# First layer's modulation vectors summed on VectorE, 512-column attention splits, new durations in the schedule

## The chip, the cores and the metric

The kernel runs on one core of a Trainium2 chip. The metric is the device time of one execution in microseconds (us). The kernel before took 1266.96 us, the median of three runs (1266.91 to 1268.06). The profiled execution, from which all rows below come, took 1268.53 us, of which the trace spans 1266.7 us. The names of the engines are those of the profile: PE is TensorE's matmul (PEld its weight load), DVE is VectorE, ACT is ScalarE, POOL is GpSimd, SP issues the DMAs.

## The reference

Two layers of a diffusion backbone over 256 latent tokens and 256 context tokens, 1024 wide. Each layer has a mixing half (three branches: windowed attention with 8 query and 2 key heads, a multi-scale pooling, a gated linear recurrence in two directions; merged by sigmoid gates) and a SwiGLU half. In the second layer only the latent tokens are carried to the end. What matters for the change:

```
mod_x = silu(c)     @ w_ada[l] + b_ada[l]     # 6 vectors of 1024, for the latent stream
mod_c = silu(c_ctx) @ w_ada[l] + b_ada[l]     # the same 6, for the context stream
h  = rms_norm(x, g_pre) * (1 + mod[1]) + mod[0]         # mixing half; vectors 4 and 3 in the SwiGLU half
x  = x + mod[2] * rms_norm(mix, g_post_mix)             # vector 5 in the SwiGLU half
p  = softmax(q k^T + mask, sink)                        # per head; 256 or 512 keys
o  = p v
h_t = a_t * h_(t-1) + b_t                               # the recurrence, forward and backward
```

All inputs and the output are float32.

## The kernel before

**Matmuls.** A float32 product is made of three reduced-precision products: each operand is split into a high part (`whi`, `h`, `b`, rounded to fp32r) and the rest (`wlo` for weights), and PE multiplies high by high, high by rest and rest by high. For weights ACT makes `whi` from the loaded tile `raw` and DVE makes `wlo = raw - whi` (`split_w`); one such pair of 128x1024 feeds 24 matmuls of 512 columns in the first layer. Activations are split in the same way by `hilo` (ACT the high part, DVE the rest). PSUM has two tags of four banks: `pm` for the large products, `pa` for everything else.

**The modulation vectors.** For one half (512 wide) of one vector, eight tiles of `w_ada` (`ra`, 128x512, eight buffers) are loaded. There are two ways to sum them. `ada_acc` does it on DVE: for each tile and each stream one SCALAR_TENSOR_TENSOR, `acc = ra * csilu + acc`; the 128 partial sums of a column, one in each partition, are then added either by four PE transposes and a DVE TENSOR_REDUCE (`ada_columns`, for vectors that are needed as columns) or by two fp32r matmuls with a matrix of ones (`ada_gate`, for the gates, after a `hilo`). `ada_rows` does it on PE: eight float32 matmuls with 32 columns of weights (`ra` with `cT`), four of them side by side in the array by `tile_position`; a DVE addition of the bias gives `ar`, and small float32 matmuls bring it into columns (`row_columns`) or spread it over the partitions (`row_gate`, with the constant `spread`). The kernel before uses `ada_rows` for six half-vectors of the first layer (vectors 3, 4 and 2), for both streams at once, and `ada_acc` for the fourteen half-vectors that are worked on in the first layer's SwiGLU half (vector 5 of the first layer, all of the second). A half-vector is one job; `tick` starts its next load between products.

**Attention.** A unit is one block of 128 queries, one pair of heads `jp` and one key head `g`: `attn_scores` (products, row maximum, exponential), `attn_trans` (scaling by the reciprocal of the sum, transposes into PSUM, `hilo` of the result), `attn_pv`. Units follow each other as a side stream beside the merge of a branch. `attn_trans` takes one `pa` bank for each of the two heads `jj` and splits it in pieces of 256 columns. The queries are split in pieces of 64 partitions by 128 columns.

**The order of the work.** No engine's order is written by hand. Every call is recorded with an estimated duration (`price`); `schedule` then plays all engines in time and fixes the order in each queue: whichever recorded operation is ready and has the lowest number comes first. Side work (recurrence, pooling, attention) is recorded with its number raised by `SIDE[l]`. On the chip each engine then works through its fixed queue in order, waiting by semaphores. The durations of `price` are thus nothing but a rule for the order. The call that issues everything stands in one line (L420), so all rows of the profile have that line.

Of the kernel before, what the change touches and what calls it, by code (L numbers as in the profile page):

```python
# [15 lines left out]
ALU = mybir.AluOpType  # L16
# [86 lines left out]
class Program:  # L103
# [114 lines left out]
    def price(self, op, method, args, kw, writes, reads):  # L218
# [10 lines left out]
        elif op.eng == "tensor":  # L229
            dt = kw["lhsT"].dtype if method == "matmul" else F32  # L230
            if method == "transpose":
                op.cost = max(n, 32) * 0.83e-3
            elif dt == F32R:
                op.cost = 0.1077 if n == 256 else 0.2145
            elif dt == BF16:
                op.cost = n * 0.4167e-3
            else:
                op.cost = max(n * 1.667e-3 / (4 if "tile_position" in kw else 1), 0.106)
# [195 lines left out]
class Builder:  # L434
# [14 lines left out]
    PAD = 80  # L449
# [50 lines left out]
    def load_constants(self, consts):  # L500
# [24 lines left out]
        self.spread = self.const([128, 2, 128], F32, "spread")  # L525
        nc.vector.tensor_copy(self.spread, self.c[:, C_SUM:C_SUM + 2].unsqueeze(2).to_broadcast([128, 2, 128]))
# [154 lines left out]
    def ada_rows(self, l, m, h, done):  # L681

        nc, w = self.nc, self.I["w_ada"][l]
        c0 = m * D + h * 512
        nc.sync.dma_start(out=self.brow[BIAS:BIAS + 1, :], in_=self.I["b_ada"][l:l + 1, c0:c0 + 512])
        raws, landings = [], []
        for k in range(8):
            raws.append(self.sb("ra", [128, 512], F32, "ra"))
            landings.append(nc.sync.dma_start(out=raws[k], in_=w[k * 128:(k + 1) * 128, c0:c0 + 512]))
            if k < 7:  # L690
                yield
        ps = self.ps("pa")
        for k in range(8):
            j = k % 4
            nc.after = landings
            nc.tensor.matmul(ps[32 * j:32 * j + 32, :], lhsT=self.cT[:, k, :], rhs=raws[k], start=k < 4, stop=k >= 4,
                             tile_position=(0, 32 * j))
            nc.after = []
        ar = self.sb("acc", [128, 512], F32, "acc")
        nc.vector.tensor_tensor(out=ar, in0=ps, in1=self.brow, op=ALU.add)  # L700
        done(ar)
        yield

    def row_columns(self, l, m, h, mods, g):
        def done(ar):
            nc = self.nc
            dst = mods[m % 3][:, h * 4:(h + 1) * 4, :]
            pc = self.ps("pa")
            for i in range(4):
                nc.tensor.matmul(pc[:, 2 * i:2 * i + 2], lhsT=ar[:, i * 128:(i + 1) * 128], rhs=self.c[:, C_SUM:C_SUM + 2],  # L710
                                 start=True, stop=True)
            p3 = pc[:, 0:8].rearrange("p (i s) -> p i s", s=2)
            if m % 3 == 0:
                nc.vector.tensor_copy(dst, p3)
            else:
                nc.vector.scalar_tensor_tensor(out=dst, in0=p3, scalar=1.0, in1=self.col(l, g, h * 4, 4).unsqueeze(2).to_broadcast([128, 4, 2]),
                                               op0=ALU.add, op1=ALU.mult)
        return self.ada_rows(l, m, h, done)

# [3 lines left out]

    def row_gate(self, l, m, h, g_post, streams, ggs):
        def done(ar):
            nc = self.nc
            for s in streams:
                gg, landing = self.gate_tile(l, h, g_post)
                ps = self.ps("pa")
                nc.after = [landing]  # L730
                nc.tensor.matmul(ps, lhsT=self.spread[:, s], rhs=ar, start=True, stop=True)
                nc.after = []
                nc.vector.tensor_tensor(out=gg, in0=ps, in1=gg, op=ALU.mult)
                ggs[s, h] = gg
        return self.ada_rows(l, m, h, done)
# [114 lines left out]
    SIDE = (40, 80)  # L850
# [241 lines left out]
    def q_out(self, ps, sl, full):  # L1092
        q = self.single(full, "q")
        self.nc.scalar.activation(q[:, sl], ps[:, sl], AF.Copy, scale=HD ** -0.5)
        self.rope(q)
        return q

# [31 lines left out]
    def attn_trans(self, st):  # L1129
# [4 lines left out]
        nkt = nk // 128  # L1134
        pts = [[self.T(dt=F32R).rearrange("p (k j q) -> p k j q", k=2, j=2) for _ in range(nkt // 2)] for _ in range(2)]
        for jj in range(2):
            p = st["p"][jj]
            nc.scalar.activation(p, p, AF.Copy, scale=rd[:, jj:jj + 1])
            ps = self.ps("pa")
            for kt in range(nkt):  # L1140
                nc.tensor.transpose(ps[:, kt * 128:(kt + 1) * 128], p[:, kt * 128:(kt + 1) * 128], self.ident)
            for i in range(nkt // 2):
                src = ps[:, i * 256:(i + 1) * 256].rearrange("p (k q) -> p k q", k=2)
                self.hilo(pts[0][i][:, :, jj, :], pts[1][i][:, :, jj, :], src)
# [16 lines left out]
    def attention(self, l, qtoks, q, kg, vg, outs):  # L1161
# [16 lines left out]
        for i in range(n + 2):  # L1178
            if i < n:
                qt, jp, g = units[i]  # L1180
                if (jp, g) == (0, 0):
                    sl = slice(qt * 128, (qt + 1) * 128)
                    two = (self.T(dt=F32R), self.T(dt=F32R))
                    qs = [[t[:, j * 128:(j + 1) * 128] for j in range(4)] for t in two]
                    for j in range(4):
                        for h in range(2):
                            a, b = slice(h * 64, (h + 1) * 64), slice((1 - h) * 64, (2 - h) * 64)
                            self.hilo(qs[h][j][a], qs[h][j][b], q[j][:, sl][a])
                state[i] = self.attn_scores(l, qt, jp, g, qs, kg)
# [225 lines left out]
    def layer_mix(self, l, hT, first):  # L1415
# [105 lines left out]
        for jp in range(2):  # L1521
            wq = self.q_weights(w_in, jp)
            for jj in range(2):
                ps = self.ps()
                self.gemm(ps, wq[jj], hT, sl)
                q[2 * jp + jj] = self.q_out(ps, sl, full)
# [260 lines left out]
```

## Time and profile before

| what | value |
|---|---|
| median of three runs | 1266.96 us |
| profiled execution | 1268.53 us |
| its span | 1266.7 us |
| PE busy | 1236.7 us (98%) |
| DVE busy | 866.6 us (68%) |
| ACT busy | 661.8 us (52%) |
| POOL busy | 36.4 us (3%) |
| moved by DMA | 200.45 MB, mean 158 GB/s |

How to read the rows below. A row of a group gives the engine, the operation, the tiles as out<-in, the shape and the count, then the busy time, the mean length of one, and the idle time just before with what ended it. Records of instructions that follow each other on one engine overlap a little, so a run of them is shorter than its count times the mean. In a row of the timeline, equal instructions are merged: start, length of the run, count. The first layer's mixing half lies at about 50 to 450 us, its SwiGLU half from there to about 830, the second layer after that.

### The profile page before, as it was taken

To read this page: it belongs to the slowest core of one execution; us is meant where nothing else is said; L and a number is where in the kernel's file an instruction comes from. 1 tells how busy PE (TensorE), PEld (TensorE's weight loads), DVE (VectorE), ACT (ScalarE), POOL (GpSimd) and SP (SyncE) were. 2 spreads that over 40 slices of the span, in tenths; PEclk is the share of its full clock that TensorE was granted. 3 is DMA by queue.
4 is the path that set the end of the run, shared out by engine and by line. 5 is a ranking of instruction groups with operands and counts; after the bars stand their busy time and mean duration, and the time that the engine had idled before them with its cause. 6 is when DMAs were issued, how large, how long until landed. Compare 5 with 4: busy or idle time off the path is not lost.

```text
span 1266.7 us, 17100 instructions
## 1 busy us (share of the span) xinstructions
PE 1236.7 (98%) x6175; PEld 1011.9 (80%) x6175; DVE 866.6 (68%) x1513; ACT 661.8 (52%) x1199; POOL 36.4 (3%) x95
## 2 busy tenths in 40 slices
PE   6999999999999999999999999999999999999997
PEld 3787877787778888888888888899876787888886
DVE  2587577778686389468477933478789977566743
ACT  4645668568633383222223322375789976566532
POOL 1000000000000020000000000120000000000000
PEclk9999999999999999999999999999999999999999
DMA  9744344343365446355658834325542475466662
GB/s 333 241 117 150 97 145 129 118 142 105 100 207 173 125 153 207 100 164 179 207 180 266 269 95 121 101 84 160 161 138 83 117 216 176 136 186 188 195 197 69
DMA packets 216700, 200.45 MB, mean 158 GB/s; under 512 B 12916, under 2 KB 171924, under 8 KB 216616
## 3 DMA queue, kind: packets, MB, share of 16 engines
q1 hardware_dynamic: 216616, 199.36, 50.9%
q8 instruction: 48, 0.79, 0.3%
q14 instruction: 36, 0.29, 0.1%
HBM read 196.18 MB, written 3.15 MB: 157 GB/s over the span
## 4 chain that ended last, share of the span: by engine, by line
PE 59%; DVE 3%; ACT 2%; issue 1%; POOL 0%; DVEq 0%; POOLq 0%; ACTq 0%
PE pm L420 47%; PE pa L420 11%; DVE t L420 1%; ACT t L420 1%; DVE wlo L420 1%; ACT junk_a L420 0%; DVE b L420 0%; POOL s L420 0%; DVE junk_v L420 0%; DVE h L420 0%; ACT hx L420 0%; ACT whi L420 0%; ACT b L420 0%; DVE hx L420 0%; ACT L420 0%
## 5 line engine op out<-in xcount | busy, mean ns | idle before, releaser
L420 PE MATMUL pm<-h,whi 128*128 128x512 f32 (+1 forms) x2096 | 609.2, 370 | 1.1 <-ACT whi L420 0.6
L420 DVE TENSOR_TENSOR wlo<-raw,whi 128x1024 fp32r<-128x1024 f32 (+1 forms) x263 | 311.2, 1187 | 189.8 <-ACT whi L420 180.4
L420 PEld LDWEIGHTS pm<-h,whi 128*128 128x128 f32 x2096 | 378.4, 190 | 70.7 <-issue 4.3
L420 PE MATMUL pm<-h,wlo 128*128 128x512 f32 (+1 forms) x1192 | 407.9, 343 | 1.4 <-DVE wlo L420 1.4
L420 ACT ACTIVATE whi<-raw 128x1024 fp32r<-128x1024 f32 (+1 forms) x263 | 268.9, 1029 | 265.5 <-PE pm L420 142.6
L420 PEld LDWEIGHTS pm<-h,wlo 128*128 128x128 f32 x1192 | 225.6, 189 | 29.2 <-DVE wlo L420 1.8
L420 PE MATMUL pm<-whi,b 128*128 128x512 f32 x456 | 165.3, 392 | 1.7 <-ACT b L420 1.7
L420 PE MATMUL pa<-whi,b 128*128 128x512 f32 x360 | 132.7, 390 | 0.0
L420 ACT ACTIVATE tm<-pm 128x512 f32<-128x512 f32 (+1 forms) x98 | 49.0, 503 | 123.2 <-PE pm L420 123.1
L420 DVE SCALAR_TENSOR_TENSOR acc<-ra,csilu,acc 128x512 f32<-128x512 f32 x140 | 101.6, 748 | 2.0 <-DMA ra<-in_w_ada_dram 0.3
L420 PEld LDWEIGHTS pm<-whi,b 128*128 128x128 f32 x456 | 85.4, 188 | 19.9 <-ACT b L420 2.5
L420 PE MATMUL pm<-wlo,b 128*128 128x512 f32 x228 | 89.4, 392 | 1.1 <-DVE wlo L420 1.1
L420 PEld LDWEIGHTS pa<-whi,b 128*128 128x128 f32 x360 | 67.4, 188 | 13.9
L420 PE MATMUL pm<-whi,h 128*128 128x512 f32 x224 | 77.0, 408 | 0.6 <-ACT whi L420 0.6
L420 PE MATMUL pa<-wlo,b 128*128 128x512 f32 x180 | 70.2, 390 | 0.0
L420 PE MATMUL pm<-b,whi 128*128 128x512 f32 x192 | 60.7, 394 | 0.0
L420 PE MATMUL pa<-consts,t 128*128 128x128 f32 x280 | 45.2, 284 | 8.3 <-DVE t L420 7.8
L420 PEld LDWEIGHTS pm<-wlo,b 128*128 128x128 f32 x228 | 42.9, 188 | 10.2 <-DVE wlo L420 1.6
L420 PEld LDWEIGHTS pm<-whi,h 128*128 128x128 f32 x224 | 41.9, 189 | 10.2 <-ACT whi L420 1.2
L420 PEld LDWEIGHTS pa<-consts,t 128*128 128x128 f32 x280 | 34.0, 145 | 19.6 <-DVE t L420 7.6
L420 DVE TENSOR_TENSOR t<-pa,t 128x256 fp32r<-128x256 f32 (+1 forms) x104 | 40.2, 418 | 11.8 <-ACT t L420 10.7
L420 POOL TENSOR_SCALAR s<-s 128x1 f32<-128x1 f32 x26 | 15.2, 584 | 1100.3 <-ACT junk_a L420 1094.3
(180 smaller groups left out, 1353.7 us busy)
## 6 DMA issues: line engine op xcount, KB each, us to landing
raw<-in_w_in_dram SPq DMA_DIRECT2D x84, 512.0 KB
ra<-in_w_ada_dram SPq DMA_DIRECT2D x160, 256.0 KB
raw<-in_w_gu_dram SPq DMA_DIRECT2D x80, 512.0 KB
raw<-in_w_down_dram SPq DMA_DIRECT2D x44, 512.0 KB
b<-in_w_ada_dram SPq DMA_DIRECT2D x32, 256.0 KB
raw<-in_w_out_dram SPq DMA_DIRECT2D x16, 512.0 KB
raw<-in_w_pool_o_dram SPq DMA_DIRECT2D x8, 512.0 KB
raw<-in_w_rnn_o_dram SPq DMA_DIRECT2D x8, 512.0 KB
```

The source lines that it names most:

```text
L420: op.fn(*op.args, **op.kw)
```

## The change

Six things are changed. (1) The six jobs of the first layer that used `ada_rows` now use `ada_columns` and `ada_gate`, as all others did; `ada_rows`, `row_columns`, `row_gate` and `spread` are gone. (2) `attn_trans` puts both heads of a unit into one set of banks and splits 512 columns at a time. (3) The queries are split for two blocks at once (`split_q`), and in the second layer two heads are rotated at once (`q_pair`). (4) `price` takes (n + 32) / 2400 us for an fp32r matmul of n columns (0.1200 for 256 and 0.2267 for 512, before 0.1107 and 0.2175) and twice the former time per column for a scan. (5) `SIDE` of the second layer goes from 80 to 40. (6) The pad in SBUF grows by 256 columns, which is the size of the constant that is gone.

```
-                op.cost = 0.1077 if n == 256 else 0.2145
+                op.cost = (n + 32) / 2400 - 0.003
...
+            if method == "tensor_tensor_scan":
+                per *= 2
...
-    PAD = 80
+    PAD = 336
...
-        self.spread = self.const([128, 2, 128], F32, "spread")
-        nc.vector.tensor_copy(self.spread, self.c[:, C_SUM:C_SUM + 2].unsqueeze(2).to_broadcast([128, 2, 128]))
...
-    SIDE = (40, 80)
+    SIDE = (40, 40)
...
+    def q_pair(self, pss):
+        q = self.B()
+        for jj in range(2):
+            nc.scalar.activation(q[:, jj * 256:(jj + 1) * 256], pss[jj][:, 256:TOK], AF.Copy, scale=HD ** -0.5)
...
+        nc.vector.stream_shuffle(sw, q, [(i + 16) % 32 for i in range(32)])
+        nc.vector.tensor_tensor(out=s3, in0=s3, in1=sin, op=ALU.mult)
...
+    def split_q(self, q, qt, full):
+            if full:
+                tiles = [self.T(dt=F32R) for _ in range(2)]
+                for j in range(4):
+                    dst = tiles[j // 2][:, j % 2 * 256:j % 2 * 256 + 256]
+                    self.hilo(dst[a], dst[b], q[j][:, qt * 128:qt * 128 + 256][a])
+            else:
+                tiles = [self.sb("ra", [128, 512], F32R, "qs") for _ in range(2)]
+                for jp in range(2):
+                    self.hilo(tiles[jp][a], tiles[jp][b], q[2 * jp][a])
...
+        banks = [self.ps("pa") for _ in range(n)]
         for jj in range(2):
             p = st["p"][jj]
             nc.scalar.activation(p, p, AF.Copy, scale=rd[:, jj:jj + 1])
-            ps = self.ps("pa")
...
-                self.hilo(pts[0][i][:, :, jj, :], pts[1][i][:, :, jj, :], src)
+            for kt in range(2 * n):
+                o = kt % 2 * 256 + jj * 128
+                nc.tensor.transpose(banks[kt // 2][:, o:o + 128], p[:, kt * 128:(kt + 1) * 128], self.ident)
+        for i in range(n):
+            self.hilo(*(pts[e][i].rearrange("p k j q -> p (k j q)") for e in range(2)), banks[i])
...
-                if (jp, g) == (0, 0):
+                if (jp, g) == (0, 0) and qt % 2 == 0:
+                    both = self.split_q(q, qt, len(qtoks) == 4)
...
-                    self.jobs.append(self.row_columns(0, m, h, self.mods, "g_pre_ffn"))
+                    self.jobs.append(self.ada_columns(0, m, h, streams, self.mods, "g_pre_ffn"))
...
-                self.jobs.append(self.row_gate(0, 2, h, "g_post_mix", streams, self.ggs))
+                self.jobs.append(self.ada_gate(0, 2, h, "g_post_mix", streams, self.ggs))
```

What this does to the queues is shown at three places. The first is PE in the first layer, at the end of the first job of six; `pm_316` and `pm_317` are the same large product, `acc_259` and `acc_260` the sums for the two streams. Before:

```order
L420 MATMUL pm_316<-h_224,wlo_319 128x512
L420 MATMUL pa_323<-ra_259,cT 32x512
L420 MATMUL pa_323<-ra_271,cT 32x512
L420 MATMUL pa_323<-ra_277,cT 32x512
L420 MATMUL pa_323<-ra_283,cT 32x512
L420 MATMUL pa_323<-ra_290,cT 32x512
L420 MATMUL pa_323<-ra_302,cT 32x512
L420 MATMUL pa_323<-ra_313,cT 32x512
L420 MATMUL pa_323<-ra_322,cT 32x512
L420 MATMUL pa_326<-t_314,whi_261 128x512
L420 MATMUL pa_326<-t_315,whi_261 128x512
```
After:

```order
L422 MATMUL pm_317<-h_223,whi_319 128x512 x2
L422 MATMUL pm_317<-h_223,wlo_320 128x512
L422 MATMUL pa_324<-consts,acc_260 128x128 x4
L422 MATMUL pa_325<-consts,acc_259 128x128 x4
L422 MATMUL pa_326<-t_315,whi_262 128x512
L422 MATMUL pa_326<-t_316,whi_262 128x512
L422 MATMUL pa_326<-t_315,wlo_263 128x512
```
The eight matmuls with `cT` have become eight transposes at the same place in the queue; the four matmuls of two columns that followed a few rows further on are gone.

The second place is DVE in the same stretch, before PE gets there: pooling (`t`), weight splits (`wlo`) and, after the change, the sums of the first job. Before:

```order
L420 TENSOR_TENSOR wlo_275<-raw_273,whi_274 128x1024
L420 TENSOR_TENSOR t_267<-t_258 128x2x270
L420 SCALAR_TENSOR_TENSOR t_247<-t_246,cols,t_247 128x512
L420 TENSOR_TENSOR wlo_281<-raw_279,whi_280 128x1024
L420 TENSOR_TENSOR t_268<-t_267 128x2x268
L420 TENSOR_TENSOR wlo_287<-raw_285,whi_286 128x1024
L420 TENSOR_TENSOR t_269<-t_268 128x2x264
L420 TENSOR_TENSOR t_270<-t_269 128x2x256
L420 TENSOR_TENSOR wlo_299<-raw_297,whi_298 128x1024
L420 TENSOR_TENSOR t_270<-t_270,consts 128x2x8 x2
L420 SCALAR_TENSOR_TENSOR t_247<-t_246,cols,t_247 128x512
```
After:

```order
L422 TENSOR_TENSOR wlo_282<-raw_280,whi_281 128x1024
L422 TENSOR_TENSOR t_269<-t_268 128x2x268
L422 TENSOR_TENSOR wlo_288<-raw_286,whi_287 128x1024
L422 TENSOR_TENSOR t_270<-t_269 128x2x264
L422 SCALAR_TENSOR_TENSOR acc_259<-ra_291,csilu,acc_259 128x512
L422 TENSOR_TENSOR t_271<-t_270 128x2x256
L422 SCALAR_TENSOR_TENSOR acc_260<-ra_291,csilu,acc_260 128x512
L422 TENSOR_TENSOR t_271<-t_271,consts 128x2x8 x2
L422 TENSOR_TENSOR wlo_300<-raw_298,whi_299 128x1024
L422 SCALAR_TENSOR_TENSOR t_283<-t_271,t_257 128x512
L422 SCALAR_TENSOR_TENSOR acc_259<-ra_303,csilu,acc_259 128x512
L422 SCALAR_TENSOR_TENSOR acc_260<-ra_303,csilu,acc_260 128x512
```
The sums stand between the weight splits, one or two at a time, the two streams in turn.

The third place is DVE in the second layer, at the second group of scans of the recurrence (the listing names a scan SCALAR_TENSOR_TENSOR; here it is those that read a `b` tile, such as `t_1861<-b_1868,t_1862`; `junk_v` is the row maximum of attention). Before:

```order
L420 TENSOR_TENSOR wlo_1983<-raw_1981,whi_1982 128x1024
L420 TENSOR_SCALAR junk_v,s_1916<-pa_1918,nsink 128x512
L420 SCALAR_TENSOR_TENSOR t_1896<-t_1902,t_1896 128x512
L420 TENSOR_SCALAR junk_v,s_1916<-pa_1920,nsink 128x512
L420 TENSOR_TENSOR t_1862<-t_1862,t_1861 128x512
L420 TENSOR_TENSOR t_1871<-t_1871,t_1870 128x512
L420 TENSOR_TENSOR t_1891<-t_1891,t_1890 128x512
L420 TENSOR_TENSOR t_1897<-t_1897,t_1896 128x512
L420 SCALAR_TENSOR_TENSOR t_1861<-b_1868,t_1862 128x512
L420 SCALAR_TENSOR_TENSOR t_1870<-b_1877,t_1871 128x256
L420 SCALAR_TENSOR_TENSOR t_1890<-b_1894,t_1891 128x512
```
After:

```order
L422 TENSOR_TENSOR wlo_1964<-raw_1962,whi_1963 128x1024
L422 SCALAR_TENSOR_TENSOR t_1897<-t_1903,t_1897 128x512
L422 TENSOR_TENSOR t_1863<-t_1863,t_1862 128x512
L422 TENSOR_TENSOR t_1872<-t_1872,t_1871 128x512
L422 TENSOR_TENSOR t_1892<-t_1892,t_1891 128x512
L422 TENSOR_TENSOR t_1898<-t_1898,t_1897 128x512
L422 SCALAR_TENSOR_TENSOR t_1862<-b_1869,t_1863 128x512
L422 SCALAR_TENSOR_TENSOR t_1871<-b_1878,t_1872 128x256
L422 SCALAR_TENSOR_TENSOR t_1891<-b_1895,t_1892 128x512
L422 SCALAR_TENSOR_TENSOR t_1871<-b_1878,t_1871,t_1872 128x256
L422 SCALAR_TENSOR_TENSOR t_1897<-b_1902,t_1898 128x256
```
Before, two row maxima of attention stand between the weight split and the scans; after, they stand behind them (from the fifth row below the piece on), and two weight splits that stood ahead of the scans now follow them: 173 splits of the whole queue stand ahead instead of 175. In both orders the next weight split after the one shown follows 24 or 25 rows further on.

## Rows read from the trace of the kernel before

**Rows 1.** the page: busy us, share of the span, instructions of each engine
```profile
PE 1236.7 (98%) x6175; PEld 1011.9 (80%) x6175; DVE 866.6 (68%) x1513; ACT 661.8 (52%) x1199; POOL 36.4 (3%) x95
```

**Rows 2.** stretches of the span: us, busy us (count) by engine, clock, DMA share, GB/s
```profile
50.00:450.00 400.00, 397.52 (x1919) 317.50 (x1919) 284.93 (x581) 233.58 (x459) 6.46 (x16) 1.00 0.44 135
350.00:400.00 50.00, 50.00 (x225) 39.28 (x224) 41.94 (x57) 16.78 (x22) 0.00 (x0) 1.00 0.56 175
475.00:825.00 350.00, 349.95 (x1593) 290.38 (x1592) 223.15 (x291) 98.87 (x135) 6.00 (x14) 1.00 0.55 171
900.00:1000.00 100.00, 94.84 (x427) 70.06 (x426) 87.60 (x180) 88.89 (x158) 0.00 (x0) 1.00 0.38 121
```

**Rows 3.** PE groups by form: busy us, mean ns | idle before
```profile
L420 PE MATMUL pa<-ra,cT 128*32 128x512 f32 x96 | 11.5, 598 | 0.0
L420 PE MATMUL pa<-acc,spread 128*128 128x512 f32 x8 | 3.8, 592 | 0.0
L420 PE MATMUL pa<-consts,acc 128*128 128x2 f32 x32 | 3.9, 244 | 0.7 <-DVE acc L420 0.7
L420 PE MATMUL pa<-consts,acc 128*128 128x128 f32 x48 | 6.7, 272 | 0.0
L420 PE MATMUL pa<-t,ones 128*128 128x512 f32 x16 | 4.3, 389 | 0.0
```

**Rows 4.** PE in order of time, around one removed group: start us, us
```profile
302.52 1.92 PE L420 MATMUL pa<-ra,cT 128*32 128x512 f32 x16
304.37 0.39 PE L420 MATMUL pa<-t,b 128*128 128x256 f32 x1
```

**Rows 5.** DVE groups by form, columns as in group 3
```profile
L420 DVE SCALAR_TENSOR_TENSOR acc<-ra,csilu,acc 128x512 f32<-128x512 f32 x140 | 101.6, 748 | 2.0 <-DMA ra<-in_w_ada_dram 0.3
L420 DVE TENSOR_REDUCE sc_m<-pa 128x4 f32<-128x512 f32 x4 | 2.7, 687 | 3.4 <-PE pa L420 3.4
L420 DVE TENSOR_TENSOR t<-acc,t 128x512 fp32r<-128x512 f32 x8 | 5.5, 688 | 0.7 <-ACT t L420 0.7
L420 DVE TENSOR_TENSOR acc<-pa,brow 128x512 f32<-128x512 f32 x6 | 4.1, 689 | 0.3 <-PE pa L420 0.2
L420 DVE TENSOR_TENSOR t<-pa,t 128x256 fp32r<-128x256 f32 x80 | 31.0, 418 | 6.3 <-ACT t L420 5.5
L420 DVE TENSOR_TENSOR t<-b,t 64x128 fp32r<-64x128 f32 x48 | 13.5, 286 | 1.1
L420 DVE TENSOR_TENSOR t<-pa,t 64x256 f32<-64x256 f32 x24 | 10.0, 418 | 5.5 <-ACT t L420 5.2
```

**Rows 6.** DVE in order of time, runs of weighted sums: start us, us
```profile
493.72 4.06 DVE L420 SCALAR_TENSOR_TENSOR acc<-ra,csilu,acc 128x512 f32<-128x512 f32 x6
...
685.96 3.12 DVE L420 SCALAR_TENSOR_TENSOR acc<-ra,csilu,acc 128x512 f32<-128x512 f32 x4
```

**Rows 7.** the stretch 475 to 825, instructions that touch acc alone
```profile
475.00:825.00 350.00, 6.69 (x48) 5.69 (x48) 97.11 (x135) 3.15 (x5) 1.00 0.55 171
```

**Rows 8.** the SP queue's waits, whole span: us in total, times, longest
```profile
SPq L420 <- DVE acc L420: 76.1, 96, 5.8
```

**Rows 9.** DVE in order of time, second layer's second scans: start us, us
```profile
962.34 2.49 DVE L420 TENSOR_TENSOR t<-t,t 128x512 f32<-128x512 f32 x4
964.75 2.91 DVE L420 TENSOR_TENSOR_SCAN t<-b,t 128x512 f32<-128x512 f32 x3
...
970.11 0.42 DVE L420 TENSOR_TENSOR t<-t,t 128x256 f32<-128x256 f32 x1
```

**Rows 10.** PE in order of time, same place: start us, us, idle before
```profile
968.25 0.73 PE L420 MATMUL pm<-whi,h 128*128 128x512 f32 x2 [0.58 <-ACT whi L420]
970.69 0.50 PE L420 MATMUL pm<-whi,b 128*128 128x512 f32 x1 [1.70 <-ACT b L420]
```

**Rows 11.** stretches around the end of the first mixing half, columns as in group 2
```profile
456.00:460.00 4.00, 2.87 (x14) 2.67 (x14) 3.65 (x4) 3.54 (x7) 2.66 (x2) 0.71 0.67 225
460.00:464.00 4.00, 4.00 (x32) 4.00 (x32) 2.22 (x3) 2.06 (x5) 0.46 (x1) 0.87 1.00 287
```

More of the change, by code (lines that the diff above doesn't have):

```diff
@@ L679, in ada_acc @@
         yield
[L681 to L691, printed above, removed]
-        ps = self.ps("pa")
[L693 to L718, printed above, removed]
     def gate_tile(self, l, h, g_post):
@@ L722, in gate_tile @@
         return gg, self.nc.sync.dma_start(out=gg, in_=self.I[g_post][l, h * 512:(h + 1) * 512].partition_broadcast(128))
[L724 to L735, printed above, removed]
     def tick(self, n=1):
@@ L1092, in q_out @@
     def q_out(self, ps, sl, full):
-        q = self.single(full, "q")
-        self.nc.scalar.activation(q[:, sl], ps[:, sl], AF.Copy, scale=HD ** -0.5)
+        q = self.B()
+        self.nc.scalar.activation(q, ps, AF.Copy, scale=HD ** -0.5)
         self.rope(q)
         return q
+    def q_pair(self, pss):
+        nc = self.nc
+        q = self.B()
+        for jj in range(2):
+            nc.scalar.activation(q[:, jj * 256:(jj + 1) * 256], pss[jj][:, 256:TOK], AF.Copy, scale=HD ** -0.5)
+        sw = self.T()
+        cos, sin = (self.c[:, o:o + 256].unsqueeze(1).to_broadcast([128, 2, 256]) for o in (C_COS, C_SIN))
+        q3, s3 = (t.rearrange("p (j q) -> p j q", j=2) for t in (q, sw))
+        nc.vector.stream_shuffle(sw, q, [(i + 16) % 32 for i in range(32)])
+        nc.vector.tensor_tensor(out=s3, in0=s3, in1=sin, op=ALU.mult)
+        nc.vector.tensor_tensor(out=q3, in0=q3, in1=cos, op=ALU.mult)
+        nc.vector.tensor_tensor(out=q, in0=q, in1=sw, op=ALU.add)
+        return q
+    def split_q(self, q, qt, full):
+        both = []
+        for h in range(2):
+            a, b = slice(h * 64, (h + 1) * 64), slice((1 - h) * 64, (2 - h) * 64)
+            if full:
[7 more added lines that the diff above has]
+                    self.hilo(tiles[jp][a], tiles[jp][b], q[2 * jp][a])
+            both.append(tiles)
+        return both
     def attn_scores(self, l, qt, jp, g, qs, kg):
@@ L1133, in attn_trans @@
         nc.vector.reciprocal(rd, st["den"])
-        nkt = nk // 128
-        pts = [[self.T(dt=F32R).rearrange("p (k j q) -> p k j q", k=2, j=2) for _ in range(nkt // 2)] for _ in range(2)]
+        n = nk // 256
+        pts = [[self.T(dt=F32R).rearrange("p (k j q) -> p k j q", k=2, j=2) for _ in range(n)] for _ in range(2)]
+        banks = [self.ps("pa") for _ in range(n)]
         for jj in range(2):
@@ L1138, in attn_trans @@
             nc.scalar.activation(p, p, AF.Copy, scale=rd[:, jj:jj + 1])
[L1139 to L1143, printed above, removed]
-                self.hilo(pts[0][i][:, :, jj, :], pts[1][i][:, :, jj, :], src)
+            for kt in range(2 * n):
[3 more added lines that the diff above has]
+            self.hilo(*(pts[e][i].rearrange("p k j q -> p (k j q)") for e in range(2)), banks[i])
         st["pT"] = pts
@@ L1180, in attention @@
                 qt, jp, g = units[i]
-                if (jp, g) == (0, 0):
[L1182 to L1188, printed above, removed]
+                if (jp, g) == (0, 0) and qt % 2 == 0:
+                    both = self.split_q(q, qt, len(qtoks) == 4)
+                o = qt % 2 * 128
+                qs = [[both[h][j // 2][:, j % 2 * 256 + o:j % 2 * 256 + o + 128] for j in range(4)] for h in range(2)]
                 state[i] = self.attn_scores(l, qt, jp, g, qs, kg)
@@ L1522, in layer_mix @@
             wq = self.q_weights(w_in, jp)
+            pss = []
             for jj in range(2):
-                ps = self.ps()
-                self.gemm(ps, wq[jj], hT, sl)
-                q[2 * jp + jj] = self.q_out(ps, sl, full)
+                pss.append(self.ps())
+                self.gemm(pss[jj], wq[jj], hT, sl)
+                if full:
+                    q[2 * jp + jj] = self.q_out(pss[jj], sl, full)
+                elif jj == 1:
+                    q[2 * jp] = self.q_pair(pss)
                 self.tick()
```

## The prediction

> **What bounds the kernel now.** I read the page first: PE is busy 1236.7 us of 1266.7, DVE 68% and ACT 52% [rows 1]. So 30.0 us of the span are without PE, and whatever is taken out of PE's queue shortens the run unless PE then waits. Next come the stretches: the reader is to see where PE waits and how full DVE is there. In the first layer's mixing half, 50 to 450 us, PE is busy 397.52 of 400 us and DVE 284.93. In the first layer's SwiGLU half, 475 to 825, PE is busy 349.95 of 350. In the second layer's mixing half, 900 to 1000, PE loses 5.16 us of 100, with DVE at 87.60 and ACT at 88.89 [rows 2]. These three stretches hold 7.7 of the 30 us; the other 22.3 lie outside them, mostly where the change does little.
>
> **What leaves PE.** Six jobs lose their eight float32 matmuls with `cT`: 96 records (two for each), 11.5 us. Two of the jobs lose two matmuls with `spread` each: 8 records, 3.8 us. Four jobs lose four matmuls of two columns: 32 records, 3.9 us [rows 3]. Together 19.2 us. The timeline confirms the largest: a group starts at 302.52 and the next matmul at 304.37, so a group keeps PE 1.85 us, six of them 11.1 [rows 4].
>
> **What comes to PE.** Four jobs, two streams, four transposes each: 32 transposes, two thirds of the 48 records that take 6.7 us, so 4.5 us. Two jobs, two streams, two matmuls with `ones`: 8, half of the 16 that take 4.3 us, so 2.15 us [rows 3]. Net 19.2 - 6.65 = 12.55 us less. A run's record ends a little after the next matmul has started (1.92 against 1.85 in rows 4), and there are more runs among the removed than among the added, so I take 12.0 us. These matmuls stood in a queue that was full on both sides, so all of it is on the path. Nothing else changes in what PE does: the attention edits move its transposes, without one more or less.
>
> **What comes to DVE, in the first layer's mixing half.** 6 jobs x 8 tiles x 2 streams = 96 weighted sums at 0.748 = 71.8 us; 8 reductions at 0.687 = 5.5; 4 rests of a split at 0.688 = 2.8; less 6 bias additions at 0.689 = 4.1 [rows 5]. That is +76.0. The wider splits give some back: of the 80 rests of 256 columns at 0.418, 48 are in the first layer and become 24 of 512, priced like the other splits of that width at 0.688: 20.1 - 16.5 = 3.6. Of the 48 query pieces at 0.286, 32 are in the first layer and become 16 of 64x256 at 0.418: 9.2 - 6.7 = 2.5 [rows 5]. So +69.9 against 400 - 284.93 = 115.1 us of idle DVE there [rows 2]: 89% full afterwards. Of the 41.94 that DVE works between 350 and 400 [rows 2], some are sums of the next half's jobs, taken ahead because DVE had time; those can go back to 475 to 825, where 126.9 us are idle.
>
> Back to back, the sums do not cost their full length: six in a row take 4.06 us, so (4.06 - 0.75) / 5 = 0.66 each. The four at 685.96, where the job has one stream and each adds to the sum before it, take 3.12, so (3.12 - 0.75) / 3 = 0.79 [rows 6]. I keep 0.748 since both patterns occur in the new queue. The Trainium skill says in "VectorE: DVE Perf Modes" (The DRAIN you can't avoid) that the next operation does not start before the pipeline is empty. By that rule 96 sums could never take less than 71.8 us; by the row of six they take 63.4, and the trace here differs from the rule. DVE would be 89% full by the one and 87% by the other.
>
> **Does PE then wait for DVE?** Two rows bound it. From 475 to 825 DVE works off 97.11 us of such jobs [rows 7] between weight splits at the same pace, and PE loses 0.05 us [rows 2]. From 900 to 1000, with DVE as full as it will be in the first layer but ACT full as well, PE loses 5.16 us in 100; over 400 us that would be 20.6. ACT has only 233.58 of 400 in the first layer [rows 2], the sums depend on nothing but a landed tile, and the queue shows them one or two at a time between weight splits, the two streams in turn. The stretch is nearer to the first row: I take +2.0, and keep 0 and +20.6. The new wait that counts is PE's at the transposes of a job. Behind them in PE's queue stand the pooling and weight products, so a late sum stops PE altogether; one sum late is 0.75 us, and six jobs end so. SP's queue also feels it: it already waits 96 times, 76.1 us in total, at most 5.8 us, for sums to free a tile [rows 8], and the loads of weights queue behind. It issues the same loads as before; I cost this at nothing, hidden by the weight tiles loaded ahead. If that cover goes, 5.8 us once is the price.
>
> **The second layer's mixing half.** Its DVE and ACT get lighter by a little: 32 rests of 256 become 16 of 512 (13.4 - 11.0 = 2.4 us on DVE), 16 query pieces become 4 of 512 columns (4.6 - 2.8 = 1.8). The order matters more. At 962 to 970.5 us DVE goes through four additions and the scans, 8.2 us in one piece [rows 9], and PE stands 1.70 us for the activation that follows from them, after 0.58 for a weight [rows 10]. The former price of a scan was 0.065 + 1.05e-3 us for a column, thus 0.60, 0.33 and 0.60 for the first three scans (512, 256 and 512 columns), together 1.53; they take 2.91 in the row [rows 9]. So PE's queue had the recurrence's products too early by 1.4 us and more. With the price doubled, those products come later in PE's queue and the scans stand ahead of attention's row maxima. Of the 5.16 us that PE loses there I take 2.5 back, the two waits of rows 10 with a little more; the bounds are 5.2 back, or 5 lost, if the two weight splits that now stand behind the 8.2 us piece come late by 2.5 us each.
>
> **Attention's 512-column splits.** The first head's transposes now wait for the second head's before any split starts, about 1.3 us later for a unit. PE has products of the merge to do meanwhile; only the last units before a drain have little cover. I take 0, with 1.5 gained or 3 lost as bounds (all that PE loses in such a stretch, or two units in each layer).
>
> **Sum.** -12.0 + 2.0 - 2.5 + 0 = -12.5. The profiled execution took 1268.53 us (span 1266.7 and 1.8 around it), so 1256.0; it stands 1.57 above the median of the runs, so the forecast for a median is 1254.5 us.
>
> **Rivals.**
> - *DVE becomes the bound of the first layer, and the run is slower.* Place: 50 to 450 us. The price is the rate of 900 to 1000, 5.16 us in 100, thus up to 20.6 us over the half; it decides from 3.0 us in 100 on, where it eats the 12.0. At the full rate the time is 1266.96 - 12.0 + 20.6 - 2.5 = 1273. For it: DVE at 89%, and PE can take no product ahead of one that waits, since its queue is in order. Against it: ACT is half idle, and rows 2 and 7 have the same mixture without loss. A pause also has an echo. From 456 to 460, after a wait, the granted clock is 0.71, the half level of 1.2 GHz for part of it, and 0.87 in the next 4 us [rows 11]: 4 x 0.29 + 4 x 0.13 = 1.7 us more. The Trainium skill in "TensorE: Matmul & The Clock Gate" (Why this matters for your kernels) warns that idle gaps between bursts of matmuls bring the clock down to half. The trace agrees at 456; from 900 to 1000, with 5.16 us of idle in short pieces, the clock stays at 1.00.
> - *The gain is eaten in part*, by late sums at the six transposes (6 x 0.75 = 4.5 in place of the 2.0) and by weights late in the second layer (5 lost in place of 2.5 won): 1254.5 + 2.5 to 1254.5 + 10.0, so 1257 to 1264.5.
> - *The waits go too.* The accurate prices empty the whole 5.2 us in the second layer and 1.5 in attention, and DVE hides everything: -12.0 - 5.2 - 1.5 = -18.7, thus 1248.3.
> - *It does not do what it says:* PE had been waiting for DVE or weights where the removed matmuls stood, so that nothing is won there. Against it: PE lost 2.48 us in those 400. It would give about 1265.
>
> **How the numbers follow.** Forecast, 1249 to 1259: 0.56. Waits go too, under 1249: 0.13. Eaten in part, 1259 to 1264.4: 0.12. Nothing won, within 0.2% (2.5 us, about what a measurement of this kernel can tell from no change): 0.08. DVE as the bound, slower: 0.11. So faster 0.81, same 0.08, slower 0.11. The range that holds 8 in 10 goes from 1246.5 (waits of which the profile shows only part go as well) to 1264.
>
> **What the profile after would show.** PE's groups with `ra,cT`, `spread` and two columns are gone, the busy time of PE falls by about 12 us; in 50 to 450 PE's idle stays under 5 us with DVE near 350 busy; the wait for the activation behind the scans is gone or under 1 us; the clock falls nowhere new. Waits of PE on `acc`, or on `wlo` between 50 and 350, would show the first rival; a longer wait on `wlo` at 930 to 1000 would show that the second layer's new order is worse.

## The result and the profile after

The changed kernel takes 1252.16 us (median of 4 runs, 1250.4 to 1253.5) against 1267.15 of before: ratio 0.988, 95% interval 0.9867 to 0.9892. Timed again beside other kernels (e5 below) it took 1253.17 against 1265.85: ratio 0.9903, interval 0.9889 to 0.9918, a somewhat smaller gain than the 0.987 to 0.989 expected of it. So the gain is 12.7 to 15.0 us; the medians of before differ by up to 1.5 us from one group of runs to the next (1265.61 to 1267.15). The forecast was 1254.5. The profiled execution took 1253.5 us (span 1251.7), 15.0 less than that of before.

The page's busy line of the changed kernel, columns as in [rows 1]:

```profile
PE 1217.6 (97%) x6079; PEld 1007.0 (80%) x6079; DVE 913.2 (73%) x1516; ACT 664.3 (53%) x1157; POOL 37.4 (3%) x95
```

PE is busy for 19.1 us less, not for the 12 expected. That column holds pace as well as work: the kernels of experiments e3, e2 and e4, which issue the same 6175 matmuls as before, show 1230.2, 1235.3 and 1235.8. So up to 6.5 us of it move without any change of work. Most of the difference to e3 is the start. The same four matmuls, and later one and the same matmul, stand here in the profiled execution of before (start us, us):

```profile
23.69 1.22 PE L420 MATMUL pm<-h,whi 128*128 128x256 f32 x4
...
53.55 0.26 PE L420 MATMUL pa<-consts,rows 112*128 112x112 f32 x1
```

and here in e3:

```profile
22.66 0.74 PE L420 MATMUL pm<-h,whi 128*128 128x256 f32 x4 [0.79 <-ACT h L420]
...
50.70 0.26 PE L420 MATMUL pa<-consts,rows 112*128 112x112 f32 x1
```

The 226 matmuls ahead of the last row are the same in both, in the same order. In the execution of before that was profiled PE ran them slower until about 27 us, and so it stood 2.85 us behind from there on; in the changed kernel the four take 0.74 as well. So about 12.2 of the 15.0 us between the two traces are the change, which fits the 12.7 of the second timing.

The PE forms of the changed kernel; the groups with `ra,cT`, `spread` and two columns of [rows 3] are gone, and these two have grown by 32 and 8 records:

```profile
L422 PE MATMUL pa<-consts,acc 128*128 128x128 f32 x80 | 10.8, 272 | 0.0
...
L422 PE MATMUL pa<-t,ones 128*128 128x512 f32 x24 | 6.6, 390 | 0.0
```

From start to next start, which leaves overlaps out, the removed groups held PE for 11.1 + 2.6 + 3.3 us, and the two grown ones rose from 4.5 to 7.8 and from 3.6 to 5.5: net -12.0.

DVE's forms, to be read against [rows 5]: the sums are there, and the rests of a split are 40 of 512 columns in place of 80 of 256:

```profile
L422 DVE SCALAR_TENSOR_TENSOR acc<-ra,csilu,acc 128x512 f32<-128x512 f32 x224 | 162.8, 747 | 2.1
L422 DVE TENSOR_TENSOR t<-pa,t 128x512 fp32r<-128x512 f32 x40 | 26.2, 683 | 0.5 <-ACT t L422 0.2
```

The stretches of [rows 2] in the changed kernel, columns as there:

```profile
50.00:450.00 400.00, 395.70 (x1919) 325.73 (x1918) 350.98 (x654) 246.83 (x458) 12.16 (x22) 1.00 0.47 143
475.00:825.00 350.00, 345.81 (x1576) 286.07 (x1575) 217.91 (x290) 106.47 (x157) 12.56 (x28) 1.00 0.51 162
900.00:1000.00 100.00, 97.46 (x474) 74.70 (x472) 90.39 (x169) 91.73 (x165) 0.00 (x0) 1.00 0.42 126
```

DVE's 350.98 is what was forecast, and PE loses 4.3 us of the 400. From 900 to 1000 it loses 2.54 in place of 5.16. But from 475 to 825 it now loses 4.19, where it lost 0.05. The end of the first layer, which comes some 15 us earlier, lies in this stretch now; it is taken apart below by 775 to 875.

The 400 us are an average of two parts, first of before, then of the changed kernel:

```profile
75.00:350.00 275.00, 273.14 (x1360) 217.17 (x1359) 200.92 (x441) 178.81 (x367) 1.20 (x5) 1.00 0.39 119
350.00:475.00 125.00, 123.37 (x624) 102.60 (x623) 84.08 (x123) 56.50 (x103) 10.02 (x16) 0.99 0.53 167
```

```profile
75.00:350.00 275.00, 272.20 (x1320) 222.22 (x1319) 266.07 (x510) 185.18 (x347) 1.27 (x5) 1.00 0.43 128
...
350.00:475.00 125.00, 123.50 (x649) 105.66 (x648) 86.27 (x125) 58.88 (x106) 9.94 (x16) 1.00 0.56 174
```

Of the 66 us that DVE has more from 50 to 450, 65 fell into these first 275, where it is now 97% full; the rest of the half has idle DVE as before. PE waits there for 2.80 us in place of 1.86.

SP's queue, where [rows 8] had 76.1 us and at most 5.8:

```profile
SPq L422 <- DVE acc L422: 134.2, 128, 11.2
```

The waits got longer. One weight then came late for ACT, which waited 3.75 us for it from 216 to 220 and had no such wait before. PE did not stop there: its idle in the first layer's half is 4.3 us.

### The profile page after: what moved, and what is told of

The parts are those of the page before. It is cut to its first block, busy times and chain, and to the rows that moved or that the text cites. A ratio compares the mean times of both kernels' runs of the same rounds, so it can differ in the third digit from the quotient of the medians.

```text
span 1251.7 us, 16846 instructions
## 1 busy us (share of the span) xinstructions
PE 1217.6 (97%) x6079; PEld 1007.0 (80%) x6079; DVE 913.2 (73%) x1516; ACT 664.3 (53%) x1157; POOL 37.4 (3%) x95
## 4 chain that ended last, share of the span: by engine, by line
PE 65%; issue 27%; DVE 2%; ACT 2%; DMA 2%; POOL 1%; SPq 0%; POOLq 0%; DVEq 0%; ACTq 0%
PE pm L422 53%; PE pa L422 13%; DVE t L422 1%; POOL s L422 1%; DVE b L422 1%; ACT junk_a L422 1%; DMA raw<-in_w_out_dram 0%; ACT whi L422 0%; DMA b<-in_w_ada_dram 0%; ACT hx L422 0%; DMA b<-in_ctx_dram 0%; DMA raw<-in_w_in_dram 0%; ACT t L422 0%; ACT h L422 0%; DVE wlo L422 0%
## 5 line engine op out<-in xcount | busy, mean ns | idle before, releaser
L422 DVE SCALAR_TENSOR_TENSOR acc<-ra,csilu,acc 128x512 f32<-128x512 f32 x224 | 162.8, 747 | 2.1
L422 PE MATMUL pm<-whi,h 128*128 128x512 f32 x224 | 74.3, 401 | 2.1 <-ACT tm L422 2.1
L422 PE MATMUL pa<-consts,t 128*128 128x128 f32 x280 | 44.5, 284 | 11.1 <-DVE t L422 8.9
L422 PE MATMUL pm<-wlo,h 128*128 128x512 f32 x112 | 44.7, 399 | 0.0
```

Source lines behind the costliest of these rows:

```text
L422: op.fn(*op.args, **op.kw)
```

## The experiments

All are timed against the kernel before on the same chip. My theory at first: the gain is PE's 12 us plus some waits of the second layer that the doubled scan price gives back, and the parts add up. The rivals are in the expectations.

**e1, the sums alone.** The kernel before with the part of the diff on the sums (`spread` and the pad go with it):

```diff
-                    self.jobs.append(self.row_columns(0, m, h, self.mods, "g_pre_ffn"))
+                    self.jobs.append(self.ada_columns(0, m, h, streams, self.mods, "g_pre_ffn"))
...
-                self.jobs.append(self.row_gate(0, 2, h, "g_post_mix", streams, self.ggs))
+                self.jobs.append(self.ada_gate(0, 2, h, "g_post_mix", streams, self.ggs))
```

> The kernel before with one part of the change alone: the six jobs sum on VectorE (splits of 256 columns, prices and side budget as before). My theory: the gain is the PE work that goes, about 12.0 us, whatever the other parts do; the waits in the second layer stay (about 5 us of PE idle between 900 and 1000), and the DVE of the first layer, with 76 us more and without the wider splits, costs PE 2 to 4 us. Time 8.5 to 11 us under before, ratio 0.991 to 0.993. Rival, the wider splits or the true prices are needed to make room on DVE: PE loses 5 us or more between 50 and 450, ratio 0.995 or more. Rival, the whole result comes from this part: ratio 0.988.

**e2, the prices and the side budget alone.**

```diff
-                op.cost = 0.1077 if n == 256 else 0.2145
+                op.cost = (n + 32) / 2400 - 0.003
...
+            if method == "tensor_tensor_scan":
+                per *= 2
...
-    SIDE = (40, 80)
+    SIDE = (40, 40)
```

> The kernel before with the two prices and the side budget alone (matrix sums stay on PE, splits of 256 columns). My theory: no busy time changes on any engine; PE's wait behind the second layer's scans shortens, 2 to 3 us gained, ratio 0.9975 to 0.9985. Rival, the true prices give back waits all over the run: 5 us or more, ratio 0.996 or less. Rival, the prices do nothing by themselves: ratio 1.000 within 0.001.

**e3, attention's wider splits alone** (`q_out`, `q_pair`, `split_q`, `attn_trans` as changed).

```diff
-            for i in range(nkt // 2):
-                src = ps[:, i * 256:(i + 1) * 256].rearrange("p (k q) -> p k q", k=2)
-                self.hilo(pts[0][i][:, :, jj, :], pts[1][i][:, :, jj, :], src)
+        for i in range(n):
+            self.hilo(*(pts[e][i].rearrange("p k j q -> p (k j q)") for e in range(2)), banks[i])
```

> The kernel before with attention's wider splits alone. My theory: DVE gets about 10 us lighter, PE keeps its instructions, and the time stays: ratio 0.9985 to 1.001. Rival, the lighter DVE in the second layer's mixing half gives PE's waits back: 2 to 3 us gained, ratio 0.998. Rival, the second head's transposes hold the first head's split: PE waits more, 1.5 to 3 us lost, ratio 1.001 to 1.0025.

**e4, all but the sums:** the edits of e2 and e3 together.

> The changed kernel with the six jobs back on PE (prices, side budget and splits as changed). My theory: the 12.0 us of PE work come back, and what is left under before is the second layer's order: 2.5 to 3 us gained, ratio 0.9975 to 0.998. Rival, the order and the splits bring more than the sums do not: 5 us or more gained, ratio 0.996 or less. Rival, they bring nothing without the sums: ratio 1.000 within 0.001.

What was measured (median; ratio to before with its interval, before 1266.21):

| kernel | us | ratio | interval |
|---|---|---|---|
| e1 sums | 1260.10 | 0.9952 | 0.9940 to 0.9964 |
| e2 prices, budget | 1275.20 | 1.0074 | 1.0059 to 1.0089 |
| e3 splits | 1267.61 | 1.0020 | 1.0007 to 1.0032 |
| e4 all but the sums | 1267.19 | 1.0008 | 0.9996 to 1.0020 |

The theory that parts add up falls: alone they give -6.1, +9.0 and +1.4 us, in sum +4.3, and together -12.7 to -15. The prices and the budget alone are a loss that none of my theories had. e1 and e3 came out as a rival of theirs had it, e4 as the rival that says nothing is gained without the sums. The 12 runs of e3 and the 12 of e4 spread over 5.9 and 6.8 us, so e3's +1.4 is small beside them.

Where e1 lost half of its 12 us, PE's timeline shows (start us, us, idle before and releaser):

```profile
169.23 0.73 PE L420 MATMUL pm<-h,whi 128*128 128x512 f32 x2 [1.66 <-ACT whi L420]
169.80 0.68 PE L420 MATMUL pa<-t,whi 128*128 128x512 f32 x2
172.69 0.50 PE L420 MATMUL pm<-h,whi 128*128 128x512 f32 x1 [2.21 <-ACT whi L420]
```

and ACT and DVE of the same kernel show why:

```profile
171.06 0.63 ACT L420 ACTIVATE b<-t 128x512 fp32r<-128x512 f32 x1 [1.37 <-DVE t L420]
171.60 1.04 ACT L420 ACTIVATE whi<-raw 128x1024 fp32r<-128x1024 f32 x1
```

```profile
166.18 1.80 DVE L420 TENSOR_TENSOR_SCAN t<-t,t 128x256 f32<-128x256 f32 x2
167.90 0.72 DVE L420 TENSOR_TENSOR_SCAN t<-t,t,t 128x256 f32<-128x256 f32 x1
```

The weight's split on ACT (171.60) ends as PE starts (172.69). It stood in ACT's queue behind an activation that waited (1.37 us) for what follows the first layer's scans. The scans' price, which I had read in the second layer alone, is at work here too. The pause also cost clock; the stretches after it:

```profile
168.00:172.00 4.00, 1.25 (x4) 0.59 (x4) 4.00 (x7) 2.63 (x5) 0.00 (x0) 1.00 0.00 0
172.00:176.00 4.00, 3.31 (x10) 2.64 (x11) 3.71 (x5) 1.27 (x2) 0.00 (x0) 0.71 0.46 133
176.00:180.00 4.00, 4.00 (x17) 3.23 (x16) 3.01 (x5) 0.00 (x0) 0.00 (x0) 0.87 0.45 132
```

Where e2 lost its 9 us, PE and ACT show in the second layer:

```profile
967.03 1.22 PE L422 MATMUL pa<-b,t 128*128 128x512 f32 x2 [3.89 <-ACT t L422]
...
971.23 1.97 PE L422 MATMUL pa<-consts,t 128*128 128x128 f32 x8 [2.31 <-ACT t L422]
```

```profile
964.47 0.42 ACT L422 ACTIVATE b<-t 128x256 fp32r<-128x256 f32 x1 [2.56 <-DVE t L422]
964.90 1.28 ACT L422 ACT_TABLE_LOAD   x1
966.20 0.69 ACT L422 ACTIVATE t<-pa,s 128x512 f32<-128x512 f32 x1
```

```profile
964.69 0.74 DVE L422 TENSOR_SCALAR_CACHE_REDUCE junk_v<-pa,nsink 128x512 bf16<-128x512 f32 x1
```

Attention's scores on PE wait for ACT's exponentials (966.20), and these stand in ACT's queue behind the activation that waits 2.56 us for the scans, and behind a table load of 1.28 us. The row maxima that they need stand behind the scans on DVE (964.69), which is the order that the prediction had counted as a gain. With the new prices and budget the planner had put the wait of [rows 10] elsewhere, and made it longer; e2 does not tell which of the three numbers does it.

The second theory: the scan's price decides in the first layer. Its rival: room on DVE decides, made by the wider splits. e5 is the changed kernel again, beside three in which pairs are joined.

> The changed kernel as it is, timed beside the next three so that they can be compared. All theories: ratio 0.987 to 0.989 to the kernel before.

**e6, sums and scan price:** e1 with

```diff
+            if method == "tensor_tensor_scan":
+                per *= 2
```

> The kernel before with the sums on VectorE and the doubled price of a scan alone (splits of 256 columns, former matmul price and side budget). New theory: sums alone gained only 6 us because in the first layer the recurrence's scans, priced at half, let weight splits fall behind them, and PE stands 4.5 us between 165 and 173 us with the clock low behind it (1.75 us more). With the scan's price right that wait goes: PE idle between 150 and 200 under 2 us, ratio 0.989 to 0.991. Rival, DVE is simply too full with the sums and the 256-column splits: the loss stays or moves within 75 to 450, ratio 0.994 or more.

**e7, sums and splits:** the edits of e1 and e3.

> The kernel before with the sums on VectorE and the wider splits, all prices and the side budget as before. New theory (the scan's price decides): the wait of 4 to 5 us behind the first layer's scans stays, ratio 0.994 to 0.996. Rival (room on DVE decides): the wider splits make the room, PE idle between 150 and 200 under 2 us, ratio 0.988 to 0.990.

**e8, sums and prices:** the edits of e1 and e2.

> The changed kernel with attention's splits of 256 columns as before (sums, both prices, side budget as changed). New theory (the scan's price decides): the first layer's mixing half is as in the changed kernel, ratio 0.988 to 0.991. Rival (room on DVE decides): PE loses 5 us or more between 75 and 450, ratio 0.993 or more.

**e9, e10 and e12, the changed kernel with one number as before:** e9 and e10 first, e12 after them, when the table below left the matmul price as the suspect for 775 to 875.

```diff
-    SIDE = (40, 40)
+    SIDE = (40, 80)
```

> The changed kernel with the second layer's side budget back at 80. The changed kernel loses 3.8 to 4.2 us of PE between 800 and 825, at the end of the first layer, where the kernel before loses 0.6; every kernel with the prices and the budget together lost 2.2 to 3.8 there. Theory: the budget of 40 does this; with 80, PE idle at that place is under 1 us and the ratio 0.986 to 0.988. Rival: the matmul price does it: the loss stays, ratio 0.990 within 0.001. Third possibility: the budget holds the second layer's waits down, and at 80 they come back between 925 and 1000 (5 us or more): ratio 0.993 or more.

```diff
-            if method == "tensor_tensor_scan":
-                per *= 2
```

> The changed kernel with the scan's former price. Theory: in the first layer PE stands 4 to 5 us behind the scans between 150 and 180 again, with the clock low for 1.7 us behind it, ratio 0.994 to 0.996. Rival: the matmul price and the wider splits have made that wait go, not the scan's price: PE idle there stays under 2 us, and the ratio is 0.990 to 0.992.

```diff
-                op.cost = (n + 32) / 2400 - 0.003
+                op.cost = 0.1077 if n == 256 else 0.2145
```

> The changed kernel with the former price of a matmul (0.2145 us for 512 columns, 0.1077 for 256). Of all kernels run, those with the new matmul price lose 2.2 to 4.2 us between 800 and 850, those with the former one 0.6, whatever the side budget. Theory: the matmul price causes that loss, and the doubled scan price with the wider splits suffices for the rest: PE idle between 800 and 850 under 1 us, the first layer's mixing half as in the changed kernel, ratio 0.985 to 0.988. Rival: the matmul price is needed in the first layer or behind the second layer's scans, and its lack costs more there than it gives back: ratio 0.993 or more.

**e11, 48 more sums on DVE,** in the changed kernel's first-layer jobs:

```diff
+            if l == 0 and m in (2, 3, 4):
+                nc.vector.scalar_tensor_tensor(out=self.junk_v, in0=raw, scalar=self.cs[:, 0, k:k + 1], in1=self.brow, op0=ALU.mult, op1=ALU.add)
```

> The changed kernel with 48 more weighted sums of 512 columns in the first layer's six jobs (results not used): 48 by 0.66 to 0.75, 32 to 36 us more on DVE. Between 75 and 450 DVE of the changed kernel is idle for 47 us, nearly all of it after 350. Theory: the queue shifts work into that rest and PE loses 0 to 4 us: ratio 0.990 to 0.994. Rival (DVE is the bound of the first layer once it is full from 75 to 350): most of the 34 us shows as waits of PE for wlo, t and acc, 10 us or more between 75 and 450, ratio 0.998 or more.

The results, and where PE lost time in each profiled execution: idle (length of the stretch less PE's busy time) + clock (over slices of 25 us, 25 times what the granted clock lacks to 1), us.

| kernel | us | ratio (interval) | 75 to 475 | 775 to 875 | 875 to 1025 |
|---|---|---|---|---|---|
| before | 1265.61 to 1267.15 | | 3.5 + 1.75 | 0.6 | 5.2 |
| changed | 1252.16 | 0.988 (0.9867 to 0.9892) | 4.3 | 4.2 + 1.75 | 2.5 |
| e5 changed again | 1253.17 | 0.9903 (0.9889 to 0.9918) | 4.0 | 3.8 | 2.4 + 1.75 |
| e1 sums | 1260.10 | above | 7.8 + 3.5 | 0.6 | 5.1 |
| e2 prices, budget | 1275.20 | above | 5.1 + 1.75 | 3.8 | 7.5 + 5.0 |
| e3 splits | 1267.61 | above | 3.1 | 0.6 | 7.1 + 5.0 |
| e4 all but sums | 1267.19 | above | 4.1 + 1.75 | 2.7 + 1.75 | 2.1 + 1.75 |
| e6 sums, scan price | 1258.06 | 0.9945 (0.9930 to 0.9961) | 7.0 | 0.6 | 5.7 + 3.5 |
| e7 sums, splits | 1259.59 | 0.9956 (0.9941 to 0.9971) | 7.4 + 1.75 | 0.6 | 7.1 + 5.0 |
| e8 sums, prices, budget | 1264.07 | 0.9988 (0.9979 to 0.9998) | 6.0 | 2.3 + 1.75 | 7.5 + 5.0 |
| e9 budget 80 | 1256.00 | 0.9919 (0.9906 to 0.9933) | 4.7 | 2.5 + 1.75 | 4.3 + 3.5 |
| e10 old scan price | 1267.25 | 1.0007 (0.9998 to 1.0017) | 9.8 | 2.2 + 3.5 | 4.8 + 3.5 |
| e12 old matmul price | 1257.28 | 0.9939 (0.9926 to 0.9953) | 6.9 | 0.6 | 5.6 + 3.5 |
| e11 48 sums more | 1277.19 | 1.0084 (1.0072 to 1.0097) | 17.4 + 10.25 | 3.8 | 2.6 + 1.75 |

Two stretches are left out: the first 75 us, and the end from 1025 on, where the idle is 9.2 us in before and 9.3 to 10.2 in the others but e4. e4's profiled execution is the slowest of its 12 (1271.64) and lost 11.9 us there, so its row stands for a slow case.

The rows that settle 775 to 875, and the second layer beside it, first of e5, then of e12:

```profile
775.00:875.00 100.00, 96.21 (x613) 86.09 (x612) 68.10 (x119) 54.51 (x110) 14.35 (x34) 1.00 0.40 113
875.00:1025.00 150.00, 147.65 (x733) 116.86 (x732) 128.53 (x226) 125.57 (x218) 0.00 (x0) 0.99 0.48 142
```

```profile
775.00:875.00 100.00, 99.36 (x628) 89.28 (x627) 69.98 (x123) 54.00 (x109) 14.16 (x34) 1.00 0.42 119
875.00:1025.00 150.00, 144.43 (x716) 114.08 (x716) 127.14 (x223) 124.27 (x216) 0.00 (x0) 0.98 0.46 135
```

What follows:

- *First layer's mixing half.* The wait behind its scans: PE idle from 150 to 200 is 4.47 us (and 1.75 of clock) in e1 and the same in e7, 2.74 in e6, 1.33 in the changed kernel, 4.80 in e10 (there without a fall of the clock). The wider splits don't remove it (e7, as expected), the scan's price does, in part, and the matmul price takes the rest (1.33 in e8, which has both prices and the former splits, 2.73 in e12). e6's time was expected at 0.989 to 0.991 and missed, since the second layer lost 0.6 + 3.5 us more than e1. Here I was right on the place and wrong on the worth. In the whole half every kernel with the sums lost 6 to 9.8 us but those with both prices and the splits (4.0 to 4.7).
- *End of the first layer, 775 to 875.* All kernels with the former matmul price lose 0.6 us there, all with the new one 2.2 to 4.2, under either side budget. e12 settles it: the matmul price costs this. It earns more elsewhere: without it the first layer loses 2.9 us more (6.9 against 4.0), the second 3.2 + 1.75 (5.6 + 3.5 against 2.4 + 1.75), and the time is 4.1 us longer than e5. e12's expected gain didn't come.
- *Second layer, 875 to 1025.* Prices alone, splits alone, and either with the sums: 7 to 7.5 + 5.0. Both together: 2 to 2.5 + 0 to 1.75, with the sums or without (e4). One number of these back, a price (e10, e12) or the budget (e9), and it is 4.3 to 5.6 + 3.5. So 8.4 of the 10.9 us by which e8 is longer than e5 lie here, and 2.0 in the first layer, where its rival had looked for them. e10 is 14.1 us longer than e5, twice what I expected: 5.8 are idle in the first layer's half, 4.2 lie here and 1.9 between 775 and 875. Why the orders come out so is not shown; the planner decides all of it at once.
- *The budget* is worth 1256.0 - 1253.2 = 2.8 us at the medians; the intervals of e9 and e5 overlap, so I count it as not shown; the theory that it costs the loss at 775 to 875 fell (2.5 + 1.75 with the budget of 80).
- *Leaving a part out of the whole* costs far more than it gives alone: sums 14.0 us (e4 - e5), splits 10.9 (e8 - e5), scan price 14.1 (e10 - e5), matmul price 4.1 (e12 - e5). The medians of before in these groups of runs differ by up to 0.9 us, which these differences carry. For the sums, 12.0 of the 14.0 are the work on PE.

No version run beats the changed kernel.

The load test needs some rows more; first the added group of e11, then the stretch from 75 to 475 us in the same kernel:

```profile
L422 DVE SCALAR_TENSOR_TENSOR junk_v<-ra,csilu,brow 128x512 bf16<-128x512 f32 x48 | 35.7, 744 | 0.0
```

```profile
75.00:475.00 400.00, 382.63 (x1800) 311.08 (x1799) 355.31 (x639) 231.80 (x438) 12.42 (x22) 0.97 0.43 129
```

35.7 us more on DVE, and the run is 24.0 us longer than e5: 0.67 for each. Of that 13.4 are PE idle (17.4 less 4.0) and 10.25 clock. DVE's idle time after 350 took 5 us of the load, not all of it as I had expected. What PE waited for between 75 and 350 (us in total, times, longest), first in e5, then in e11:

```profile
PE pm L422 <- DVE wlo L422: 0.8, 1, 0.8
```

```profile
PE pm L422 <- DVE wlo L422: 8.4, 7, 1.7
PE pa L422 <- DVE t L422: 3.2, 3, 1.9
```

DVE ends 11.6 of the 15.8 us that PE waits there. The rival "DVE is the bound" holds as soon as something is added. Part of it may come through the loads, since the added sums hold the `ra` tiles longer: ACT waited once 7.5 us for a weight to land. That part is not taken apart.

## Why the prediction came out right, step by step

**What leaves and comes to PE: right.** -12.0 us forecast, -12.0 by the rows from start to start. e1 alone would have hidden it: there half was lost again to waits.

**What comes to DVE: right.** +69.9 us forecast for 50 to 450, +66.0 measured. The prediction set its row of six sums (4.06 us) against the Trainium skill, "VectorE: DVE Perf Modes" (The DRAIN you can't avoid). That section adds in the same place that an operation which is not held starts earlier, so the row does not contradict it.

**Waits for DVE in the first layer: the size right, the reason wrong.** +2.0 forecast; idle rose by 0.8 (3.5 to 4.3), and 1.75 us of clock that the execution of before lost at 450 was not lost. The step that failed is "The stretch is nearer to the first row". I had averaged DVE over 400 us, 89% full; it is 97% full over 275 and slack behind. With the sums and less than the other parts, PE loses 6 to 9.8 us there (e1, e6, e7, e8, e10, e12), and with 36 us more 17.4 + 10.25 (e11). The first rival, put at 0.11, was near. What kept it away is the order of the first layer's queues that the two prices and the wider splits give together (4.0 to 4.7); I had looked for the prices' effect in the second layer only.

**The second layer: the size right, the cause wrong.** -2.5 forecast, -2.6 measured (5.16 to 2.54). But "With the price doubled, those products come later in PE's queue and the scans stand ahead of attention's row maxima" is not why: with the prices alone the same place loses 7.5 + 5.0 (e2). It takes the wider splits with both prices (e4, e5 against e8, e10, e12) and, by one profile of each kernel, the budget of 40 (e9). In the changed kernel one wait of more than 0.5 us is left, for an activation again (PE, columns as before):

```profile
954.02 0.50 PE L422 MATMUL pm<-whi,h 128*128 128x512 f32 x1 [2.07 <-ACT tm L422]
```

**Attention's splits at 0: right alone** (+1.4 by e3, within the bounds of -1.5 to +3), wrong in company: the step asked what they do to the order of before, from 1.3 us a unit that no run measured by itself. In the changed order they are worth 10.9 us (e8 - e5).

**What was missing:** 3.6 us idle, and in one execution 1.75 of clock, between 775 and 875, from the matmul price. I had costed this price nowhere, and "the clock falls nowhere new" was wrong by it.

**The sum held because errors cancelled:** -12.0 + 0.8 - 2.6 + 3.6 = -10.2 for PE's work and idle, against about -12.2 between the traces without the start. The stretches left out change little: idle is +1.0 from 1025 on, and -1.2 in the first 75 us when e3 stands for a start without the delay. The clock does not explain the other 2 us either, since its falls took 3.5 us in both traces. They lie inside PE's busy time, and I have not placed them. That the sum hit is therefore in part luck. A sum of parts tried one by one, as e1 to e3 are, would have said +4.3 us.

## What to carry to other kernels

Where a planner orders full queues, test an edit by leaving it out of the whole as well as by trying it alone: here the parts alone sum to a loss, and the whole gains 12.7 us or more. Before adding work to an engine, read its load over the stretch in which it is fed, not over the stage: the 89% forecast were 97% there, and 36 us more cost 24. A pause of PE is dearer than its idle time where the clock falls behind it.

## What the hardware showed unexpectedly

The granted clock falls after a wait in one execution and not after the same wait in the next. The changed kernel in its two profiles, the first, then e5:

```profile
800.00:825.00 25.00, 20.81 (x119) 16.97 (x118) 19.62 (x33) 18.67 (x43) 10.61 (x24) 0.98 0.22 62
825.00:850.00 25.00, 25.00 (x202) 25.00 (x201) 17.98 (x29) 14.87 (x27) 0.00 (x0) 0.95 0.35 103
950.00:975.00 25.00, 22.46 (x127) 17.47 (x126) 24.54 (x63) 23.57 (x55) 0.00 (x0) 1.00 0.30 89
```

```profile
800.00:825.00 25.00, 21.21 (x127) 17.45 (x127) 19.48 (x34) 19.47 (x45) 10.00 (x24) 1.00 0.22 64
825.00:850.00 25.00, 25.00 (x211) 25.00 (x210) 20.12 (x36) 14.79 (x26) 0.14 (x2) 1.00 0.41 119
950.00:975.00 25.00, 22.97 (x124) 18.06 (x125) 23.74 (x60) 23.23 (x55) 0.00 (x0) 0.93 0.35 105
```

PE's idle is nearly the same, 4.19 and 3.79 us, then 2.54 and 2.03; each fall costs about 1.75 us (25 times the 0.07 that the clock lacks in these rows), and it moves from one place to the other. One profile can therefore not place a microsecond or two of clock. In e11, with many waits close together, the fall is deep:

```profile
212.00:216.00 4.00, 1.17 (x4) 0.31 (x3) 4.00 (x6) 2.65 (x5) 0.00 (x0) 0.92 0.01 1
216.00:220.00 4.00, 3.80 (x9) 3.07 (x10) 4.00 (x7) 0.00 (x0) 0.00 (x0) 0.50 0.78 211
```

After 2.83 us of idle in these four, the clock is at 0.50 in the next row, which is 1.2 GHz. The Trainium skill, "TensorE: Matmul & The Clock Gate" (Why this matters for your kernels), warns of idle gaps between bursts of matmuls for this; the trace agrees here, with 0.50. In e5 3.79 us of idle between 800 and 825, in pieces of at most 1.57, passed without a fall; what decides it is not shown.
